# One core, one decoder block: the triangular inverse's upper two steps take two chunks in one product, and the decay masks come from GpSimd selections

## The chip, the cores and the metric

The kernel runs on one core of a Trainium2 chip. The metric is the device time of the whole program in microseconds (us). The time before is the median of three runs, 2971.11 us (2970.61 to 2977.27).

Engines: PE is TensorE (matrix products; PEld is its weight load), DVE is VectorE, ACT is ScalarE, POOL is GpSimd, SP issues the DMAs. Each runs its own instructions in order and waits on semaphores of the others.

## What is computed

A decoder trunk of one layer on 2048 tokens of width 1024: gated DeltaNet attention (8 heads of 128) and a 4-head attention over 256 memory tokens, side by side, then a squared-ReLU MLP, each with a residual and a layer norm. The change touches DeltaNet only. Cut to what matters:

```
gc = cumsum(g)                                     # within a chunk
decay = exp(where(causal, gc[:, None] - gc[None, :], -inf))
lower = where(strict, (beta * k) @ k.T * decay, 0)
a_mat = eye + lower
u = solve(a_mat, beta * v);  w = solve(a_mat, beta * k * exp(gc))
attn_qk = (q @ k.T) * decay
# then the scan over chunks with state S:
v_new = u - w @ S;  o = q_decay @ S + attn_qk @ v_new
S = S * exp(gc_last) + k_decay.T @ v_new
```

The reference uses chunks of 64 tokens. The kernel uses chunks of 128, which gives the same result, and needs the inverse of a unit lower triangular 128x128 matrix for every chunk and head.

## The kernel before

Tokens come in NB = 4 blocks of TB = 512, each of NC = 4 chunks of P = 128. For a block the kernel runs DeltaNet and memory attention, the output projection, norm 1, the MLP (its second product as a seven-product scheme on 2x2 blocks) and norm 2. Big products are in fp32r with each operand split into a high and a low part, three passes for one product (`mm3`). Weights are split by ACT (`CAST whl`) and DVE (`TENSOR_TENSOR whl`). Block 0 splits the input weights and stores them, the later blocks load them split.

DeltaNet is a pipeline over heads: at step t the kernel records `gdn_b(t-2)` (the scan with the state), `gdn_a(t-1)` (decay, k·k, q·k, the inverse) and `dense(t)` (the projections q, k, v, z, named aq, ak, av, az in the trace). In `gdn_a`, `gb` is a DMA that lays the row of cumulated gates over all partitions; DVE adds a mask (`m_l`, `m_at`: 0 or ±1e30) and ACT takes the exponential. This gives `dl` and `at`, which DVE multiplies with the products `pkq`.

`invert` gets `L` = `dl`, four chunks side by side. First DVE inverts the 16-row diagonal blocks by columns (`Xc`, `Bc`, `Lc`). Then three steps double the block: 16 to 32, 32 to 64 and 64 to 128 rows. Each step has two products with a copy between them, -X2 · L21 · X1:

- the first product goes into bank `pq`, ACT copies it to `Q`;
- the second, with the other inverse as stationary operand, goes into bank `pp`, and DVE (by scaling with -1) writes the result to its place.

Buffers: `XB`, `LB` (16 to 32), `L32`, `X32` (32 to 64), `L` itself and `X64` (64 to 128); `ZT` and `Z` hold the 32-row inverses, transposed and not; `Y` is the result, whose first reader is `pc<-R,Y` in `gdn_b`. In the two upper steps each of the four chunks is a product of its own with a stationary operand of 64 columns. The trace names a buffer without its number: L32 is `L`, X32 and X64 are both `X`.

All of this is only recorded. `Recorder.issue` then sets the order on all engines: it is a list scheduler that gives each operation a duration (`cost`) and picks, on the engine that is free first, the ready operation recorded first. So a change of costs or dependences moves instructions everywhere. All recorded instructions are issued from one line, L320. `rec.buf(..., bufs, ...)` limits how many tiles of a tag live at once; `.part(key)` says that parts of a tile are independent of each other.

Of the kernel before, what the change touches and what calls it, by code (L numbers as in the profile page):

```python
# [134 lines left out]
class Recorder:  # L135
# [47 lines left out]
    @staticmethod  # L183
    def cost(o, name, wr, rd, args, kw):
        e = o.eng
        shapes = [r.shape for r in wr] + [r.shape for r in rd]
        n = max([_prod(s[1:]) for s in shapes] or [1])
        if e == "PE":
            rhs = kw.get("rhs", args[2])
            mo, n = _prod(args[1].shape[1:]), _prod(rhs.shape[1:])  # L190
            f32 = name == "transpose" or isinstance(rhs, Ref) and rhs.buf.dtype == F32
            o.load = 4 + 0.84 * mo
            o.last = 2.4 + 0.8334 * n if f32 else 13.4 + 0.4167 * n
            if name == "transpose":
                return o.last
            if f32:
                return o.last + max(o.last, o.load)
            return o.last
        psum = any(r.buf.psum for r in rd + wr)
        if e == "SP":  # L200
            o.extra = 1700 + _prod(wr[0].shape if wr else rd[0].shape) * 4 / 300.0
            return 450
        scal = [v for v in args[2:] if isinstance(v, Ref)] if name.startswith("tensor_scalar") else []
        scal += [v for k, v in kw.items() if k in ("scalar", "scalar1", "scale", "bias") and not isinstance(v, (int, float))]
        if e == "ACT":
            n = _prod((wr[0]).shape[1:])
# [12 lines left out]

    def issue(self):  # L220
# [116 lines left out]
def hybrid_layer(  # L337
# [24 lines left out]
    nc = tc.nc  # L362
# [6 lines left out]
    cst = ctx.enter_context(tc.tile_pool(name="cst", bufs=1))  # L369
# [31 lines left out]
    m_at = cst.tile([P, P], F32, name="m_at")  # L401
    nc.gpsimd.memset(m_at, 0.0)
    m_l = cst.tile([P, P], F32, name="m_l")
    nc.gpsimd.memset(m_l, 0.0)
    nc.gpsimd.affine_select(out=m_at, in_=m_at, compare_op=ALU.is_ge, fill=-1e30,
                            base=0, pattern=[[1, P]], channel_multiplier=-1)
    nc.gpsimd.affine_select(out=m_l, in_=m_l, compare_op=ALU.is_gt, fill=1e30,
                            base=0, pattern=[[-1, P]], channel_multiplier=1)
# [19 lines left out]
    rec = Recorder(nc, tc)  # L428
    BN_DIM = nc.vector.BN_STATS_DIM
    nc = rec  # L430
# [154 lines left out]
    def gates(b, T):  # L585
# [26 lines left out]
        t = small("gt", sh, 1)  # L612
# [3 lines left out]
        d = small("gd", sh, 1)  # L616
# [6 lines left out]
        p = small("gp", sh, 1)  # L623
# [36 lines left out]
        gct = small("gct", [32, P], 2)  # L660
# [69 lines left out]
    def invert(L, par):  # L730

        Lq = small("Lq", [P, 32, NC], 2)
        for q in range(4):
            r = slice(32 * q, 32 * q + 32)
            nc.vector.tensor_copy(Lq[r].rearrange("p f c -> p c f"), L[r, :, 32 * q:32 * q + 32])
            nc.gpsimd.tensor_copy(inv[par % NI]["LB"][r, :, 32 * q:32 * q + 16], L[r, :, 32 * q:32 * q + 16])
        for p in range(2):
# [9 lines left out]
        for j in range(15):  # L747
# [3 lines left out]
                                    in1=Lc[:, j:j + 1].to_broadcast([P, w, NC]), op=ALU.mult)  # L751
# [7 lines left out]
        XB, LB, L32, X32, X64, Q = (inv[par % NI][n] for n in ("XB", "LB", "L32", "X32", "X64", "Q"))  # L759
        Y = slot("Y", "s%d" % par)  # L760
        Y3 = v4(Y)
        nc.gpsimd.memset(Y, 0.0)
# [2 lines left out]
            nc.scalar.copy(out=XB[r, :, r], in_=Z[r])  # L765

        W = P - 16
        pq = bank("pq", "ga%d" % par)[:W, :64].rearrange("p (c f) -> p c f", c=NC)
        for c in range(NC):
            nc.tensor.matmul(pq[:, c], LB[:, c, :W], ZT[:, c, 16:32], start=True, stop=True)  # L770
        nc.scalar.copy(out=Q[:W, :, :16], in_=pq)
        pp = bank("pp", "ga%d" % par)[:W, :64].rearrange("p (c f) -> p c f", c=NC)
        for c in range(NC):
            nc.tensor.matmul(pp[:, c], XB[:, c, :W], Q[:, c, :16], start=True, stop=True)
        nc.vector.tensor_tensor(out=ZT[:W, :, 16:32], in0=ZT[:W, :, 16:32], in1=pp, op=ALU.subtract)

        Z = small("Z32", [P, NC, 32], 2)
# [6 lines left out]
        pq = bank("pq", "ga%d" % par)[:64, :P].rearrange("p (c f) -> p c f", c=NC)  # L784
        for c in range(NC):
            nc.tensor.matmul(pq[:, c], L32[:, c], ZT[:, c], start=True, stop=True)
        nc.scalar.copy(out=Q[:64, :, :32], in_=pq)
        p32 = bank("pp", "ga%d" % par)
        pp = p32[:64, :P].rearrange("p (c f) -> p c f", c=NC)
        for c in range(NC):  # L790
            nc.tensor.matmul(pp[:, c], X32[:, c], Q[:, c, :32], start=True, stop=True)
        t32 = Lq[:32].rearrange("p f c -> p (f c)")
        nc.vector.transpose(t32, p32[:32, :P])
        for p in range(2):
            nc.vector.tensor_scalar_mul(Y3[64 * p:64 * p + 32, :, 64 * p + 32:64 * p + 64],
                                        pp[32 * p:32 * p + 32], -1.0)
        nc.vector.tensor_scalar_mul(X64[32:64, :, :32], t32.rearrange("p (c f) -> p c f", c=NC), -1.0)

        pq = bank("pq", "ga%d" % par)[:64, :2 * P].rearrange("p (c f) -> p c f", c=NC)
        for c in range(NC):  # L800
            nc.tensor.matmul(pq[:, c], L[:, c, :64], Y3[:, c, 64:], start=True, stop=True)
        nc.scalar.copy(out=Q[:64], in_=pq)
        pp = bank("pp", "ga%d" % par)[:64, :2 * P].rearrange("p (c f) -> p c f", c=NC)
        for c in range(NC):
            nc.tensor.matmul(pp[:, c], X64[:, c], Q[:, c], start=True, stop=True)
        nc.vector.tensor_scalar_mul(Y3[:64, :, 64:], pp, -1.0)
        return Y3

    def sumsq(p3, nm):
# [7 lines left out]
    def gdn_a(h, r, G):  # L817
# [23 lines left out]
        nc.vector.tensor_tensor(out=at3, in0=gb3, in1=m_at.unsqueeze(1).to_broadcast([P, NC, P]), op=ALU.add)  # L841
# [427 lines left out]
```

## Time and profile before

| | |
|---|---|
| median of the runs | 2971.11 us |
| profiled execution | 2967.86 us, its span 2966.1 us |
| granted TensorE clock | 0.998 |
| PE MATMUL pq<-ZT,L and pq<-Y,dl (first products of the two steps) | 256 passes each |
| PE MATMUL pp<-Q,X (their second products) | 512 passes |
| chain that ended last, by line | PE af 40%, PE ao 6%, PE pp 2%, PE pq 2% |

The span is the time from the first to the last instruction. A row of the timeline gives start, duration, engine, line, operation, output<-inputs and the shape; x8 merges eight instructions, and a bracket holds the idle time ahead of it and who ended it. A row of the groups gives count, busy us, mean ns, and the idle time ahead. An fp32 matmul shows as two passes per product. Matmuls are pipelined, so their durations overlap.

### The profile page before, as it was taken

How to read it: one execution, taken by the hardware profiler on the slowest of the kernel's cores; microseconds unless marked ns; L12 is line 12 of the kernel's file. 1: busy time of each engine (PE TensorE's matmuls, PEld its weight loads, DVE VectorE, ACT ScalarE, POOL GpSimd, SP SyncE). 2: the span in 40 equal slices, each digit the busy share in tenths (PEclk: the TensorE clock that was granted, in tenths of full speed). 3: DMA queues.
4: the chain of work that ended last, by engine and by line, in shares of the span. 5: the costliest groups of instructions: out<-in, count | busy, mean ns of one | idle time of the engine just before them, and what ended most of it. 6: DMA issues, size and time to landing. Idle time of an engine off the chain costs nothing.

```text
span 2966.1 us, 43768 instructions
## 1 busy us (share of the span) xinstructions
PE 2922.6 (99%) x15172; PEld 2410.1 (81%) x15172; DVE 2178.7 (73%) x5568; ACT 1518.2 (51%) x3582; POOL 342.1 (12%) x872
## 2 busy tenths in 40 slices
PE   8999999999999999999999999999999999999998
PEld 6888778888788878888888878888878887888886
DVE  7899887666888876665588777755668877675667
ACT  6666535444456652554545555344454556444443
POOL 2222100000122201000022220000001221000000
PEclk9999999999999999999999999999999999999999
DMA  8655577555733322544473333244456333324444
GB/s 283 238 192 178 192 237 234 194 190 181 278 136 121 121 100 79 158 146 137 154 258 135 122 111 100 89 144 148 149 168 244 125 122 111 100 86 149 145 146 135
DMA packets 127709, 469.84 MB, mean 158 GB/s; under 512 B 14464, under 2 KB 16896, under 8 KB 109056
## 3 DMA queue, kind: packets, MB, share of 16 engines
q1 hardware_dynamic: 126912, 467.00, 47.1%
q8 instruction: 119, 1.95, 0.3%
q14 instruction: 102, 0.84, 0.1%
q10 hardware_dynamic: 576, 0.06, 0.0%
HBM read 402.97 MB, written 64.03 MB: 157 GB/s over the span
## 4 chain that ended last, share of the span: by engine, by line
PE 81%; DVE 8%; ACT 7%; DMA 2%; issue 2%; POOL 1%; ACTq 0%; POOLq 0%; DVEq 0%
PE af L320 40%; PE ao L320 6%; PE az L320 5%; PE av L320 5%; PE ak L320 4%; PE aq L320 4%; PE amq L320 3%; PE pc L320 3%; DVE y L320 2%; PE pp L320 2%; PE pq L320 2%; PE po L320 2%; PE pkq L320 1%; DVE whl L320 1%; PE sps L320 1%
## 5 line engine op out<-in xcount | busy, mean ns | idle before, releaser
L320 DVE TENSOR_TENSOR whl<-wraw,whl 128x1024 fp32r<-128x1024 f32 (+1 forms) x446 | 541.4, 1216 | 462.6 <-ACT whl L320 460.9
L320 ACT CAST whl<-wraw 128x1024 fp32r<-128x1024 f32 (+1 forms) x446 | 466.6, 1046 | 371.7 <-PE af L320 202.6
L320 PE MATMUL af<-Thi,whl 128*128 128x512 f32 (+1 forms) x2304 | 649.8, 366 | 4.6 <-DVE whl L320 2.7
L320 PEld LDWEIGHTS af<-Thi,whl 128*128 128x128 f32 x2304 | 416.8, 189 | 76.0 <-DVE whl L320 3.7
L320 PE MATMUL af<-whl,xh 128*128 128x512 f32 x1536 | 474.8, 390 | 1.3 <-DVE whl L320 0.7
L320 PE MATMUL af<-Tlo,whl 128*128 128x512 f32 (+1 forms) x1152 | 421.1, 366 | 0.0
L320 PE MATMUL af<-whl,xl 128*128 128x512 f32 x896 | 346.0, 389 | 0.0
L320 PEld LDWEIGHTS af<-whl,xh 128*128 128x128 f32 x1536 | 287.8, 188 | 67.4 <-ACT whl L320 3.7
L320 PEld LDWEIGHTS af<-Tlo,whl 128*128 128x128 f32 x1152 | 217.3, 189 | 35.1
L320 PE MATMUL ao<-whl,ch 128*128 128x512 f32 x768 | 245.2, 397 | 0.3 <-DVE y L320 0.3
L320 ACT ACTIVATE rl<-af 128x512 f32<-128x512 f32 x128 | 76.5, 598 | 277.1 <-PE af L320 275.2
L320 PEld LDWEIGHTS af<-whl,xl 128*128 128x128 f32 x896 | 168.2, 188 | 34.4
L320 PE MATMUL aq<-Thi,whl 128*128 128x512 f32 x512 | 181.7, 412 | 7.2 <-ACT Thi L320 7.2
L320 PE MATMUL az<-Thi,whl 128*128 128x512 f32 x512 | 177.3, 406 | 1.1 <-DVE whl L320 1.1
L320 PE MATMUL av<-Thi,whl 128*128 128x512 f32 x512 | 176.6, 406 | 0.0
L320 PE MATMUL ak<-Thi,whl 128*128 128x512 f32 x512 | 173.5, 403 | 0.0
L320 PEld LDWEIGHTS ao<-whl,ch 128*128 128x128 f32 x768 | 143.1, 188 | 27.9 <-issue 1.4
L320 PE MATMUL ao<-whl,cl 128*128 128x512 f32 x384 | 156.2, 407 | 0.0
L320 DVE SCALAR_TENSOR_TENSOR y<-y,af 128x512 f32<-128x512 f32 x224 | 146.2, 677 | 8.7 <-PE af L320 8.7
L320 POOL MEMSET Y<- 128x512 f32 x32 | 16.8, 525 | 1037.9 <-PE af L320 921.0
L320 PEld LDWEIGHTS aq<-Thi,whl 128*128 128x128 f32 x512 | 94.7, 190 | 22.3 <-ACT Thi L320 7.2
L320 PEld LDWEIGHTS az<-Thi,whl 128*128 128x128 f32 x512 | 93.9, 189 | 17.3 <-DVE whl L320 1.5
(251 smaller groups left out, 5747.2 us busy)
## 6 DMA issues: line engine op xcount, KB each, us to landing
wraw<-in_w_ff_dram SPq DMA_DIRECT2D x224, 512.0 KB, 4.0
whl<-wsc SPq DMA_DIRECT2D x108, 1024.0 KB, 4.8
wraw<-tsc SPq DMA_DIRECT2D x128, 512.0 KB, 3.4
wsc<-whl SPq DMA_DIRECT2D x36, 1024.0 KB, 4.8
wraw<-in_w_out_dram SPq DMA_DIRECT2D x48, 512.0 KB, 4.2
wraw<-in_w_in_dram SPq DMA_DIRECT2D x35, 512.0 KB, 5.8
wq<-in_w_ff_dram SPq DMA_DIRECT2D x64, 256.0 KB, 4.4
tsc<-wq SPq DMA_DIRECT2D x64, 256.0 KB, 3.8
```

What stands on the lines that cost most here:

```text
L320: o.fn(*[res(a) for a in o.args], **{k: res(v) for k, v in o.kw.items()})
```

## The change

The two upper steps hold two chunks in one stationary operand of 128 columns with two diagonal blocks: chunk c in one block and chunk c + 2 in the other. So `L32`, `X32`, `X64` and the new `LP` (the lower left 64x64 blocks of L) are 128 columns wide and two deep. The moving operand has the two chunks on different partitions: `ZP` (in the space of `Lq`) for the first step, `YP` for the second. There are two products where there were four. Copies that filled one operand are split in halves between POOL and DVE, and results of `pp` between DVE and ACT. The masks `m_l` and `m_at` go; two POOL selections write `dl` and `at` from `gb`. Two POOL costs in the scheduler change, and `gct` has one buffer in place of two.

```
         if name == "tensor_copy":
-            return 119 + 3.34 * n
+            return 120 + 1.3 * n
+        if name == "affine_select":
+            return 180 + 0.9 * n
...
-        for n, f in (("XB", P), ("LB", P), ("L32", 64), ("X32", 64), ("X64", 64), ("Q", 64)):
-            d[n] = rec.buf(cst, (P, NC, f), F32, n + str(i), 1, n)
+        for n, shape in (("XB", (NC, P)), ("LB", (NC, P)), ("L32", (2, P)), ("X32", (2, P)), ("X64", (2, P)),
+                         ("LP", (2, P)), ("Q", (2 * P,))):
+            d[n] = rec.buf(cst, (P,) + shape, F32, n + str(i), 1, n)
...
         for p in range(2):
-            nc.gpsimd.tensor_copy(inv[par % NI]["L32"][64 * p + 32:64 * p + 64, :, 32 * p:32 * p + 32],
-                                  L[64 * p + 32:64 * p + 64, :, 64 * p:64 * p + 32])
+            rows = slice(64 * p + 32, 64 * p + 64)
+            nc.gpsimd.tensor_copy(L32[rows, :, 64 * p:64 * p + 32].part((0, p)), L[rows, 0:2, 64 * p:64 * p + 32])
+            nc.vector.tensor_copy(L32[64 * p:64 * p + 32, :, 64 * p + 32:64 * p + 64].part((1, p)),
+                                  L[rows, 2:4, 64 * p:64 * p + 32])
+        nc.gpsimd.tensor_copy(LP[64:, :, :64].part(0), L[64:, 0:2, :64])
+        nc.vector.tensor_copy(LP[:64, :, 64:].part(1), L[64:, 2:4, :64])
...
+        for p in range(2):
+            odd = slice(64 * p + 32, 64 * p + 64)
+            nc.vector.tensor_copy(ZP[64 * p:64 * p + 32].part(2 * p + 1), ZT[odd, 2:4])
+            nc.scalar.copy(out=ZP[odd].part(2 * p), in_=ZT[odd, 0:2])
         nc.vector.transpose(Z.rearrange("p c f -> p (c f)"), ZT.rearrange("p c f -> p (c f)"))
         for p in range(2):
-            nc.vector.tensor_copy(X32[32 * p:32 * p + 32, :, 32 * p:32 * p + 32], Z[64 * p:64 * p + 32])
-            nc.gpsimd.tensor_copy(X64[32 * p:32 * p + 32, :, 32 * p:32 * p + 32], Z[32 * p:32 * p + 32])
+            for u, eng in ((0, nc.gpsimd), (1, nc.vector)):
+                q = quads[2 * p + u]
+                eng.tensor_copy(X32[q, :, q].part((u, p)), Z[64 * p:64 * p + 32, 2 * u:2 * u + 2])
...
-        for c in range(NC):
-            nc.tensor.matmul(pq[:, c], L32[:, c], ZT[:, c], start=True, stop=True)
+        for c in range(2):
+            nc.tensor.matmul(pq[:, c], L32[:, c], ZP[:, c].part(0, 1, 2, 3), start=True, stop=True)
...
-        for c in range(NC):
-            nc.tensor.matmul(pq[:, c], L[:, c, :64], Y3[:, c, 64:], start=True, stop=True)
-        nc.scalar.copy(out=Q[:64], in_=pq)
+        YP = small("YP", [P, 2, 64], 1)
+        nc.vector.tensor_copy(YP[:64].part(1), Y3[64:, 2:4, 64:])
+        nc.scalar.copy(out=YP[64:].part(0), in_=Y3[64:, 0:2, 64:])
+        for c in range(2):
+            nc.tensor.matmul(pq[:, c], LP[:, c], YP[:, c], start=True, stop=True)
+        nc.scalar.copy(out=Q[:, P:].rearrange("p (c f) -> p c f", c=2).part(2), in_=pq)
...
-        nc.vector.tensor_scalar_mul(Y3[:64, :, 64:], pp, -1.0)
+        nc.vector.tensor_scalar_mul(Y3[:64, 2:4, 64:], pp[64:], -1.0)
+        nc.scalar.activation(Y3[:64, 0:2, 64:], pp[:64], AF.Copy, scale=-1.0)
...
-        nc.vector.tensor_tensor(out=dl3, in0=gb3, in1=m_l.unsqueeze(1).to_broadcast([P, NC, P]), op=ALU.add)
+        nc.gpsimd.affine_select(out=dl3, in_=gb3, compare_op=ALU.is_gt, fill=1e30,
+                                base=0, pattern=[[0, NC], [-1, P]], channel_multiplier=1)
```

Two places show how the change moves instructions. The first is PE in block 1, head 2: the end of its 32-to-64 step and its 64-to-128 step, before:

```order
L320 MATMUL pp<-Q,X_157 64x32 x4
L320 MATMUL av<-Thi,whl 128x512
L320 MATMUL av<-Tlo,whl 128x512
L320 MATMUL av<-Thi,whl 128x512 x2
L320 MATMUL av<-Tlo,whl 128x512
L320 MATMUL av<-Thi,whl 128x512
L320 MATMUL pq<-Y,dl 64x64 x4
L320 MATMUL av<-Thi,whl 128x512
L320 MATMUL av<-Tlo,whl 128x512
L320 MATMUL av<-Thi,whl 128x512
L320 MATMUL pp<-Q,X_162 64x64 x4
```

And PE now, at the 64-to-128 step of the same head:

```order
L322 MATMUL ak<-Tlo,whl 128x512
L322 MATMUL ak<-Thi,whl 128x512
L322 MATMUL av<-Thi,whl 128x512
L322 MATMUL av<-Tlo,whl 128x512
L322 MATMUL av<-Thi,whl 128x512
L322 MATMUL pq<-YP,LP 128x64 x2
L322 MATMUL av<-Thi,whl 128x512
L322 MATMUL av<-Tlo,whl 128x512
L322 MATMUL av<-Thi,whl 128x512
L322 MATMUL pp<-Q,X_152 128x64 x2
```

Four products of 64 columns are two of 128; between the two steps stand eleven rows of projection where five stood, and from the last product to the first reader of Y (pc<-R,Y) it is 18 rows where it was 14.

The second place is POOL, where the selections for a head stand ahead of the copies of the head before it, again in block 1; before:

```order
L320 TENSOR_TENSOR vbs<-betah,rk 128x4
L320 TENSOR_TENSOR bh<-beta,rk 128x4
L320 MEMSET Y 128x512
L320 TENSOR_TENSOR bh<-bh,rk 128x4
L320 TENSOR_TENSOR nbe<-bh,neg 128x4
L320 COPY X_162<-Z_9944 32x4x32 x2
```

And POOL now:

```order
L322 AFFINE_SELECT dl<-gb 128x512
L322 AFFINE_SELECT at<-gb 128x512
L322 MEMSET Y 128x512
L322 TENSOR_SCALAR ss<-ss 128x8
L322 TENSOR_SCALAR m_10098<-oss 128x4
L322 TENSOR_TENSOR rk<-ss,mhalf 128x4
L322 TENSOR_TENSOR m_10098<-m_10098,e_9226 128x4
L322 COPY X_147<-Z_10114 32x2x32
L322 TENSOR_TENSOR ro<-m_10098,mhalf 128x4
L322 COPY X_147<-Z_10114 32x2x32
L322 COPY X_152<-Z_10114 32x2x32 x2
```

The two selections have come in ahead of Y's memset, and the copies of X now hold X32's first half (X_147), which stood on DVE, besides X64's (X_152).

More of the change, by code (lines that the diff above doesn't have):

```diff
@@ L400, in hybrid_layer @@
                             base=0, pattern=[[1, P]], channel_multiplier=-1)
[L401 to L408, printed above, removed]
     half = cst.tile([P, 2], F32, name="half")
@@ L659, in gates @@
         nc.tensor.transpose(pt[:32, :P], gcf, ident)
[L660 removed]
+        gct = small("gct", [32, P], 1)
         nc.vector.tensor_copy(gct, pt[:32, :P])
@@ L758, in invert @@
         nc.vector.transpose(ZT.rearrange("p c f -> p (c f)"), Z.rearrange("p c f -> p (c f)"))
-        XB, LB, L32, X32, X64, Q = (inv[par % NI][n] for n in ("XB", "LB", "L32", "X32", "X64", "Q"))
+        XB, LB, X32, X64, Q = (inv[par % NI][n] for n in ("XB", "LB", "X32", "X64", "Q"))
         Y = slot("Y", "s%d" % par)
@@ L767, in invert @@
         W = P - 16
+        Q16 = Q[:W, :64].rearrange("p (c f) -> p c f", c=NC).part(0)
         pq = bank("pq", "ga%d" % par)[:W, :64].rearrange("p (c f) -> p c f", c=NC)
@@ L770, in invert @@
             nc.tensor.matmul(pq[:, c], LB[:, c, :W], ZT[:, c, 16:32], start=True, stop=True)
-        nc.scalar.copy(out=Q[:W, :, :16], in_=pq)
+        nc.scalar.copy(out=Q16, in_=pq)
         pp = bank("pp", "ga%d" % par)[:W, :64].rearrange("p (c f) -> p c f", c=NC)
         for c in range(NC):
-            nc.tensor.matmul(pp[:, c], XB[:, c, :W], Q[:, c, :16], start=True, stop=True)
+            nc.tensor.matmul(pp[:, c], XB[:, c, :W], Q[:, c * 16:(c + 1) * 16].part(0), start=True, stop=True)
@@ L779, in invert @@
         for p in range(2):
-            nc.vector.tensor_copy(X32[32 * p:32 * p + 32, :, 32 * p:32 * p + 32], Z[64 * p:64 * p + 32])
-            nc.gpsimd.tensor_copy(X64[32 * p:32 * p + 32, :, 32 * p:32 * p + 32], Z[32 * p:32 * p + 32])
+            for u, eng in ((0, nc.gpsimd), (1, nc.vector)):
+                q = quads[2 * p + u]
+                eng.tensor_copy(X32[q, :, q].part((u, p)), Z[64 * p:64 * p + 32, 2 * u:2 * u + 2])
+        for p in range(2):
+            for u, eng in ((0, nc.gpsimd), (1, nc.vector)):
+                q = quads[2 * u + p]
+                eng.tensor_copy(X64[q, :, q].part((u, p)), Z[quads[p], 2 * u:2 * u + 2])
@@ L792, in invert @@
[L792 to L800, printed above, removed]
-            nc.tensor.matmul(pq[:, c], L[:, c, :64], Y3[:, c, 64:], start=True, stop=True)
@@ L802, in invert @@
-        nc.scalar.copy(out=Q[:64], in_=pq)
-        pp = bank("pp", "ga%d" % par)[:64, :2 * P].rearrange("p (c f) -> p c f", c=NC)
-        for c in range(NC):
-            nc.tensor.matmul(pp[:, c], X64[:, c], Q[:, c], start=True, stop=True)
-        nc.vector.tensor_scalar_mul(Y3[:64, :, 64:], pp, -1.0)
+        pq = bank("pq", "ga%d" % par)[:, :64].rearrange("p (c f) -> p c f", c=2)
+        for c in range(2):
+            nc.tensor.matmul(pq[:, c], L32[:, c], ZP[:, c].part(0, 1, 2, 3), start=True, stop=True)
@@ new lines, in invert @@
+        nc.scalar.copy(out=Q[:, 64:P].rearrange("p (c f) -> p c f", c=2).part(1), in_=pq)
+        pb = bank("pp", "ga%d" % par)[:, :64]
+        pp = pb.rearrange("p (c f) -> p c f", c=2)
+        for c in range(2):
+            nc.tensor.matmul(pp[:, c], X32[:, c], Q[:, 64 + c * 32:64 + (c + 1) * 32].part(1), start=True, stop=True)
+        tr = Lq.rearrange("p f c -> p (f c)")[:64, 64:].part("t")
+        nc.vector.transpose(tr, pb[:64])
+        for p in (1, 0):
+            o = Y3[64 * p:64 * p + 32, :, 64 * p + 32:64 * p + 64]
+            nc.vector.tensor_scalar_mul(o[:, 2:4], pp[quads[2 * p + 1]], -1.0)
+            nc.scalar.activation(o[:, 0:2], pp[quads[2 * p]], AF.Copy, scale=-1.0)
@@ new lines, in invert @@
+        tr = tr.rearrange("p (c f) -> p c f", c=2)
+        for u in range(2):
+            nc.vector.tensor_scalar_mul(X64[quads[2 * u + 1], :, quads[2 * u]].part((u, 2)), tr[quads[u]].part("t"), -1.0)
+        YP = small("YP", [P, 2, 64], 1)
+        nc.vector.tensor_copy(YP[:64].part(1), Y3[64:, 2:4, 64:])
+        nc.scalar.copy(out=YP[64:].part(0), in_=Y3[64:, 0:2, 64:])
+        pq = bank("pq", "ga%d" % par)[:, :P].rearrange("p (c f) -> p c f", c=2)
+        for c in range(2):
+            nc.tensor.matmul(pq[:, c], LP[:, c], YP[:, c], start=True, stop=True)
@@ L807, in invert @@
+        nc.scalar.copy(out=Q[:, P:].rearrange("p (c f) -> p c f", c=2).part(2), in_=pq)
+        pp = bank("pp", "ga%d" % par)[:, :P].rearrange("p (c f) -> p c f", c=2)
+        for c in range(2):
+            nc.tensor.matmul(pp[:, c], X64[:, c], Q[:, P + c * 64:P + (c + 1) * 64].part(2), start=True, stop=True)
+        nc.vector.tensor_scalar_mul(Y3[:64, 2:4, 64:], pp[64:], -1.0)
+        nc.scalar.activation(Y3[:64, 0:2, 64:], pp[:64], AF.Copy, scale=-1.0)
         return Y3
@@ L840, in gdn_a @@
         at3 = v4(at)
-        nc.vector.tensor_tensor(out=at3, in0=gb3, in1=m_at.unsqueeze(1).to_broadcast([P, NC, P]), op=ALU.add)
+        nc.gpsimd.affine_select(out=at3, in_=gb3, compare_op=ALU.is_ge, fill=-1e30,
+                                base=0, pattern=[[0, NC], [1, P]], channel_multiplier=-1)
         for c in range(NC):
```

7 lines of the change are left out of this document (2 added, 5 removed).

## The prediction

> **What bounds the kernel now.** I read the page first, then stretches of time, then the timeline of single products.
>
> ```profile
> span 2966.1 us, 43768 instructions
> PE 2922.6 (99%) x15172; PEld 2410.1 (81%) x15172; DVE 2178.7 (73%) x5568; ACT 1518.2 (51%) x3582; POOL 342.1 (12%) x872
> PE 81%; DVE 8%; ACT 7%; DMA 2%; issue 2%; POOL 1%; ACTq 0%; POOLq 0%; DVEq 0%
> ```
>
> TensorE is busy for 2922.6 of 2966.1 us and holds 81% of the chain that ended last. So time that leaves TensorE leaves the kernel, as long as another engine doesn't hold the stage. The stage that is changed is DeltaNet, at four places, one for each block of 512 tokens:
>
> ```profile
> 130.00:300.00 170.00, 167.99 (x1018) 137.61 (x1017) 153.79 (x555) 115.25 (x365) 44.89 (x121) 1.00 0.52 179
> 800.00:1080.00 280.00, 278.50 (x1643) 229.77 (x1643) 225.39 (x881) 166.51 (x564) 64.26 (x187) 1.00 0.35 124
> 1560.00:1800.00 240.00, 236.97 (x1427) 193.93 (x1426) 190.24 (x752) 138.71 (x477) 56.14 (x155) 0.99 0.32 115
> 2290.00:2540.00 250.00, 246.92 (x1486) 202.22 (x1484) 200.66 (x799) 146.32 (x503) 54.15 (x141) 1.00 0.32 113
> ```
>
> The columns after the stretch are PE, weight loads, DVE, ACT, POOL, granted clock, DMA share and GB/s. PE is full in all four (277 of 280 us and alike). But DVE is busy for 153.79 of 170 us (90%) in block 0, which still splits its weights into high and low parts, and for 79 to 80% in the other three. ACT is at 58 to 68%, POOL at 22 to 26%.
>
> "Busy" on PE hides something, since durations of matmuls overlap. What a product really takes is read from the starts around it. Here are PE's rows of one head in block 1, around a 32-to-64 product and a 64-to-128 product of before:
>
> ```profile
> 911.81 0.40 PE L320 MATMUL av<-Thi,whl 128*128 128x512 f32 x1
> 912.14 0.65 PE L320 MATMUL pq<-ZT,L 128*64 128x32 f32 x8
> 912.72 0.50 PE L320 MATMUL av<-Thi,whl 128*128 128x512 f32 x1
> 913.06 0.40 PE L320 MATMUL av<-Tlo,whl 128*128 128x512 f32 x1
> 913.29 0.40 PE L320 MATMUL av<-Thi,whl 128*128 128x512 f32 x1
> ...
> 916.17 0.40 PE L320 MATMUL av<-Thi,whl 128*128 128x512 f32 x1
> 916.49 0.68 PE L320 MATMUL pq<-Y,dl 128*64 128x64 f32 x8
> 917.10 0.50 PE L320 MATMUL av<-Thi,whl 128*128 128x512 f32 x1
> 917.44 0.40 PE L320 MATMUL av<-Tlo,whl 128*128 128x512 f32 x1
> ```
>
> A projection's pass takes 0.23 us (913.06 to 913.29). From the pass ahead of a group to the second one behind it lie 1.25 us (911.81 to 913.06) and 1.27 us (916.17 to 917.44); less two passes of 0.23, the groups take **0.79 and 0.81 us**. x8 is four chunks in two fp32 passes each. The loads show how little of that is work:
>
> ```profile
> 912.14 0.54 PEld L320 LDWEIGHTS pq<-ZT,L 128*64 128x64 f32 x8 [0.36 <-DVE Bc L320]
> 919.18 0.59 PEld L320 LDWEIGHTS ptv<-ident,cv 128*128 128x128 f32 x4
> 919.18 0.39 PE L320 MATMUL az<-Thi,whl 128*128 128x512 f32 x1
> 919.41 0.60 PE L320 MATMUL ptv<-ident,cv 128*128 128x128 f32 x4
> 919.77 0.47 PE L320 MATMUL az<-Thi,whl 128*128 128x512 f32 x1
> 920.08 0.39 PE L320 MATMUL az<-Tlo,whl 128*128 128x512 f32 x1
> ```
>
> The eight 64-column loads start with their group (912.14), though the pass ahead started at 911.81; the four 128-column loads of ptv start at 919.18, together with the pass ahead, and are hidden under it. One 64-column load lasts 0.138 us in the groups below, so the eight start 0.057 us apart ((0.54-0.138)/7), 0.46 us in all. The other 0.33 us are edges: the array is run dry on entry and on the way back. The 128-wide group of four passes takes 919.18 to 920.08 = 0.90 us, less 0.46: **0.44 us**, without edges. A product of 128 columns with two passes says the same:
>
> ```profile
> 947.43 0.39 PE L320 MATMUL ak<-Thi,whl 128*128 128x512 f32 x1
> 947.66 0.38 PE L320 MATMUL pc<-R,Y 128*128 128x128 f32 x2
> 947.80 0.48 PE L320 MATMUL ak<-Thi,whl 128*128 128x512 f32 x1
> 948.11 0.39 PE L320 MATMUL ak<-Tlo,whl 128*128 128x512 f32 x1
> ```
>
> 0.68 us less 0.46 is 0.22 for two passes, 0.44 for four.
>
> **The change part by part: PE.** Each head loses four 64-column groups of eight passes (two at 0.79, two at 0.81 us) and gets four 128-column groups of four passes. Their moving operand is 32 or 64 wide, so the loads set the pass: twice 0.057, four times, is 0.46; the rows above give 0.44. I take 0.45. Gain: 2 x 0.34 + 2 x 0.36 = **1.40 us a head**, 44.8 us for 32 heads (4 blocks of 8):
>
> ```profile
> L320 PEld LDWEIGHTS pq<-ZT,L x256: 132/138/232, 102.0 to 2548.7; 128*64 128x64 f32 x128
> L320 PE MATMUL pp<-Q,X x512: 213/222/271, 104.3 to 2554.5; 128*64 128x64 f32 x86, 128*64 128x32 f32 x85
> ```
>
> 256 passes are 32 heads of eight. The 112-column groups of the 16-to-32 step stay as they are.
>
> A rule speaks against this: the Trainium skill, "TensorE: Matmul & The Clock Gate", section "LDWEIGHTS (loading the stationary operand)", has the load as columns / 1.2 ns, so by its figures, as an estimate, eight 64-column loads and four 128-column ones are both 0.43 us and nothing is won. The 0.057 us above agrees with it per load. The skill's "TensorEngine Tiling (Array Packing)", "Key Properties", says that going from one tiling mode to another drains TensorE, and counts 128x64 as a mode of its own; the late loads at 912.14 agree. By the first rule alone the sum would be 0, by both 44.8 us.
>
> **DVE.** These rows go or shrink:
>
> ```profile
> L320 DVE TENSOR_TENSOR dl<-gb,m_l 128x512 f32<-128x512 f32 x32 | 21.8, 682 | 0.1
> L320 DVE TENSOR_TENSOR at<-gb,m_at 128x512 f32<-128x512 f32 x32 | 21.8, 683 | 0.2 <-PE pc L320 0.2
> L320 DVE COPY X<-Z 32x128 f32<-32x128 f32 x64 | 15.5, 242 | 1.1
> L320 DVE STREAM_TRANSPOSE Lq<-pp 32x128 f32<-32x128 f32 x32 | 9.7, 302 | 18.2 <-PE pp L320 18.1
> L320 DVE TENSOR_SCALAR Y<-pp 32x128 f32<-32x128 f32 x64 | 16.9, 263 | 0.7
> L320 DVE TENSOR_SCALAR X<-Lq 32x128 f32<-32x128 f32 x32 | 7.3, 229 | 0.6
> L320 DVE TENSOR_SCALAR Y<-pp 64x256 f32<-64x256 f32 x32 | 13.3, 415 | 12.4 <-PE pp L320 11.9
> ```
>
> Out go 2 x 0.68 for the masks and, in the steps, 2 x 0.242 + 0.302 + 2 x 0.263 + 0.229 + 0.415 = 1.96: 3.32 us. In come ten SBUF copies (two L32, one LP, two ZP, two X32, two X64, one YP). Most move half of the 0.242 us row's elements; between a mere fixed part and the whole row I take 0.22, so 2.2. With the narrower transpose (0.27), two Y at 0.22, two X64 scalings at 0.20 and the last Y at 0.29 that is 3.6. DVE **gains 0.3 us a head** (bounds -0.2 to +0.6). In blocks 1 to 3 a fifth of DVE is free, which hides it. In block 0, 16.2 of 170 us are free: a head takes some 35 us (eight in the second stretch's 280), so 3.3 us are free per head, and 1.40 + 0.3 eat half of them. There I count on half the gain.
>
> **ACT and POOL.**
>
> ```profile
> L320 ACT COPY Y<-ZT 32x128 f32<-32x128 f32 x128 | 37.7, 295 | 19.4 <-DVE ZT L320 17.8
> L320 ACT COPY vt<-pc 128x128 f32<-128x128 f32 x128 | 34.2, 267 | 126.2 <-PE pc L320 125.7
> L320 POOL COPY X<-Z x64: 279/285/1318, 102.1 to 2549.4; 32x128 f32<-32x128 f32 x64
> L320 POOL MEMSET Y<- 128x512 f32 x32 | 16.8, 525 | 1037.9 <-PE af L320 921.0
> L407 POOL TENSOR_SCALAR_AFFINE_SELECT m_l<-m_l 128x128 f32<-128x128 f32 x1 | 0.3, 292 | 0.0
> ```
>
> ACT gets two ZP, one YP and three Y pieces, 0.25 to 0.27 us each by the first two rows, less narrower Q copies: about 1.4 us on some 24 busy of 35 in block 0 (115.25 of 170). Free time hides that. POOL gets two selections per head. A 128x128 one took 0.292 us; four times the elements is 0.29 (all fixed) to 1.17 us (all per element). The 128x512 memset took 0.525 us, so I take 0.6, 1.2 for both. POOL is three quarters free, and in the order shown the selections stand well ahead of the products they feed. The masks' wait for gb moves from DVE's queue to POOL's. Behind it stand Y's memset and the ss/rk scaling of the next head; these had the slack of POOL's free time so far.
>
> What is late next is the inversion's own chain. Two copy stages are new in it (ZP ahead of the first product, YP ahead of the third), 0.25 us each, and X32's first half now comes from POOL. The order has the last product 18 rows ahead of its first reader pc<-R,Y (14 before), so most is covered by projection passes. I charge 0.15 us of new PE wait per head; bounds 0 (all hidden) and 0.6 (both stages and their hand-overs exposed).
>
> **Sum**, against the profiled execution's 2967.86 us: blocks 1 to 3, 24 x 1.40 = 33.6, less 24 x 0.15 = 3.6; block 0, half of 8 x 1.40 = 5.6. Gain 35.6, so 2932.3. The runs' median is 2971.11, 3.3 above; on it I forecast **2936 us**, 1.2% less.
>
> **Rivals.** (1) *Loads only*: the edges come from the semaphore wait ahead of each group, not from its width, and stay. Against it: pc<-R,Y waits for DVE's R as well and has no edge. PE then gains nothing: 2971. (2) *The other engines hold the stage*: block 0 gives nothing since DVE is full, and in blocks 1 to 3 the whole 0.6 us of the new stages shows: 24 x 0.80 = 19.2, less DVE's 0.3 x 8 = 2.4 in block 0. That gives 2954. For it: 7% of the chain on ACT, 8% on DVE. (3) *Slower, by X32 on POOL*: the second product of the 32-to-64 step now waits for two POOL copies of Z. They took 0.285 us in the median but 1.318 at most. If they ran at 1.3 each, 2.6 us would stand against the 1.1 us that the first product (0.45), Q's copy and their hand-overs cover; with 0.24 for the transpose that is 1.75 us of wait a head. It decides from 1.40 on: 32 x 0.35 = 11, so 2982. Against it: a median near the minimum. The skill's "GPSIMD Engine Reference", section "Specifications", names VectorE's two-port modes and its two-input instructions as sharing the SBUF interface; the 1.318 us agree, though nothing in this trace shows the cause.
>
> **How the numbers follow.** Forecast 0.68, (1) 0.07, (2) 0.20, (3) 0.05. The forecast's own range runs from everything gained (2971 - 45 = 2926, and up to 6 us of the 43.5 us that PE idles now, since another order may lose fewer) to half its waits more. I put 2920 to 2957, which takes in (2) and leaves out (1) and (3). About 0.3%, 9 us, is what a measurement of this kernel tells from no change. Faster 0.88, same 0.07, slower 0.05.
>
> **What would show it.** Right: groups "128*128 128x32 x4" and "128x64 x4" whose neighbours stand 0.45 + 0.46 us apart, loads hidden under the pass ahead, PE's passes down by 512, DVE over 93% busy in block 0. Wrong: edges that stay, PE waits on POOL X or ACT YP of over 0.3 us a head, or a DeltaNet stage as long as before.

## The result, and the profile after

| | before | after |
|---|---|---|
| median of the runs | 2970.86 us (2968.97 to 2977.27, 4 runs) | 3010.55 us (3007.82 to 3013.75, 4 runs) |
| profiled execution | 2967.86 us | 3008.75 us |

The ratio is 1.013, with an interval of 1.0111 to 1.0149. The change makes the kernel 40 us slower where 35 us less had been forecast.

The page of the kernel after, engine totals and the chain that ended last by engine:

```profile
span 3007.0 us, 43426 instructions
PE 2907.9 (97%) x14660; PEld 2401.7 (80%) x14660; DVE 2220.4 (74%) x5792; ACT 1562.0 (52%) x3774; POOL 380.9 (13%) x1029
PE 68%; DVE 18%; ACT 7%; issue 3%; POOL 2%; DMA 2%; DVEq 0%; POOLq 0%; ACTq 0%; SPq 0%
```

PE has its 512 passes less and is busy for 15 us less, but the span is 41 us longer. PE's share of the chain fell from 81 to 68%, and DVE's rose from 8 to 18%. The same four stretches of DeltaNet show where (columns after the stretch: PE, weight loads, DVE, ACT, POOL, granted clock, DMA share, GB/s):

```profile
130.00:300.00 170.00, 160.46 (x905) 132.86 (x903) 152.58 (x564) 119.64 (x394) 50.48 (x144) 0.99 0.50 175
800.00:1080.00 280.00, 266.98 (x1472) 220.27 (x1472) 226.14 (x869) 170.07 (x589) 73.72 (x216) 0.99 0.38 136
1560.00:1800.00 240.00, 226.62 (x1264) 187.91 (x1264) 201.41 (x810) 144.91 (x504) 62.62 (x193) 0.99 0.35 125
2290.00:2540.00 250.00, 235.37 (x1307) 195.25 (x1306) 205.24 (x815) 149.55 (x520) 63.12 (x183) 0.99 0.35 127
```

PE, which was full (278.50 of 280), now idles 13 of 280 us in block 1. DVE is hardly fuller than before there (226.14 against 225.39), so the stage isn't short of DVE's time.

Below, *length* is DeltaNet's time in a block on PE, from the last pass of one MLP to the first pass of the next, and *stall* is length less PE's work. The work counts each pass at what it takes between undisturbed neighbours (0.227 us for 512 columns in fp32r, an fp32 pass the longer of its load and its stream), plus 0.32 us for the edges of a 64-column group. It is a model and holds to a few us; the lengths are measured.

| block | 0 | 1 | 2 | 3 |
|---|---|---|---|---|
| length before, us | 430.8 | 386.5 | 390.5 | 389.1 |
| length after | 445.7 | 396.7 | 396.8 | 397.9 |
| PE's work before / after | 408.9 / 398.1 | 378.3 / 367.2 | 378.3 / 367.2 | 378.3 / 367.2 |
| stall before / after | 21.9 / 47.6 | 8.2 / 29.4 | 12.2 / 29.6 | 10.8 / 30.7 |

By this model the work falls by 44 us over the four blocks, as forecast, and the stall rises by 84. Now PE in block 1, head 2 of the kernel after, with DVE and ACT beside it, in the timeline:

```profile
925.39 0.63 PE L322 MATMUL ak<-Thi,whl 128*128 128x512 f32 x2
...
925.86 0.53 PE L322 MATMUL pp<-Q,X 128*128 128x32 f32 x4
...
926.22 0.48 PE L322 MATMUL ak<-Tlo,whl 128*128 128x512 f32 x1
...
926.54 0.63 PE L322 MATMUL ak<-Thi,whl 128*128 128x512 f32 x2
...
927.63 0.69 DVE L322 SCALAR_TENSOR_TENSOR cq<-th,cq 128x512 f32<-128x512 f32 x1
...
928.24 0.23 DVE L322 STREAM_TRANSPOSE Lq<-pp 64x64 f32<-64x64 f32 x1
...
928.51 0.23 DVE L322 TENSOR_SCALAR Y<-pp 32x64 f32<-32x64 f32 x1
...
929.00 0.22 ACT L322 ACTIVATE Y<-pp 32x64 f32<-32x64 f32 x1
...
929.30 0.39 PE L322 MATMUL av<-Thi,whl 128*128 128x512 f32 x1
...
929.84 0.68 DVE L322 TENSOR_TENSOR kq<-cq,kq 128x512 fp32r<-128x512 f32 x1
930.55 0.22 DVE L322 TENSOR_SCALAR Y<-pp 32x64 f32<-32x64 f32 x1
...
930.80 0.21 ACT L322 ACTIVATE Y<-pp 32x64 f32<-32x64 f32 x1 [1.58 <-DVE Y L322]
...
931.04 0.29 ACT L322 COPY YP<-Y 64x128 f32<-64x128 f32 x1
931.28 0.22 DVE L322 COPY YP<-Y 64x128 f32<-64x128 f32 x1
...
931.62 0.52 PEld L322 LDWEIGHTS pq<-YP,LP 128*128 128x128 f32 x4 [2.36 <-ACT YP L322]
```

The group itself is as forecast: from 925.39 to 926.54 lie 1.15 us with three projection passes of 0.23, which leaves **0.46 us** for pp, without edges. But its result is ready at about 926.4 and DVE takes it at 928.24, since it is behind with other work. Then four pieces of Y run in turns, DVE, ACT, DVE, ACT, and two copies to YP follow. PE starts its last projection pass at 929.30 and has nothing until 931.62. From pp to pq it is 5.8 us; before it was 2.18 for the same head, from this row to pq at 916.49:

```profile
914.31 0.65 PE L320 MATMUL pp<-Q,X 128*64 128x32 f32 x8
```

The waits of PE's weight loads over the whole kernel after (us in total, times, longest):

```profile
PEld pq L322 <- ACT YP L322: 26.1, 20, 2.4
PEld pc L322 <- DVE R L322: 15.9, 21, 1.9
PEld ptv L322 <- ACT Y L322: 12.6, 20, 1.7
PEld ptq L322 <- ACT kd L322: 11.5, 14, 2.4
PEld pp L322 <- ACT Q L322: 10.7, 18, 1.4
PEld pc L322 <- DVE state L322: 9.1, 17, 1.4
```

And the same waits before:

```profile
PEld pp L320 <- ACT Q L320: 9.5, 15, 1.0
PEld ptq L320 <- ACT kd L320: 5.3, 14, 1.7
PEld pc L320 <- DVE state L320: 3.2, 6, 0.8
PEld pc L320 <- DVE R L320: 2.3, 8, 0.4
PEld ptv L320 <- DVE Y L320: 1.0, 2, 0.6
```

The largest is the new copy stage, but over half of the rise in these rows stands at products that the change doesn't touch (pc, ptv, ptq). PE is ahead of the others at many places, not only at YP.

### The profile page after: what moved, and what is told of

The parts are those of the page before. It is cut to its first block, busy times and chain, and to the rows that moved or that the text cites. A ratio compares the mean times of both kernels' runs of the same rounds, so it can differ in the third digit from the quotient of the medians.

```text
span 3007.0 us, 43426 instructions
## 1 busy us (share of the span) xinstructions
PE 2907.9 (97%) x14660; PEld 2401.7 (80%) x14660; DVE 2220.4 (74%) x5792; ACT 1562.0 (52%) x3774; POOL 380.9 (13%) x1029
## 4 chain that ended last, share of the span: by engine, by line
PE 68%; DVE 18%; ACT 7%; issue 3%; POOL 2%; DMA 2%; DVEq 0%; POOLq 0%; ACTq 0%; SPq 0%
PE af L322 40%; PE ao L322 6%; PE az L322 4%; PE av L322 3%; PE aq L322 2%; DVE y L322 2%; PE pc L322 2%; DVE cq L322 2%; PE ak L322 2%; PE amq L322 2%; DVE whl L322 1%; DVE Lq L322 1%; PE po L322 1%; ACT jq L322 1%; DVE dl L322 1%
## 5 line engine op out<-in xcount | busy, mean ns | idle before, releaser
L322 DVE SCALAR_TENSOR_TENSOR y<-y,af 128x512 f32<-128x512 f32 x224 | 146.5, 678 | 10.1 <-PE af L322 10.1
L322 PEld LDWEIGHTS av<-Thi,whl 128*128 128x128 f32 x512 | 96.4, 191 | 17.3
```

The source lines that it names most:

```text
L322: o.fn(*[res(a) for a in o.args], **{k: res(v) for k, v in o.kw.items()})
```

## The experiments

**1 and 2: masks or steps.** One kernel puts only the masks of the change into the kernel before, the other takes only the masks out of the kernel after (two mask additions on DVE again; scratch tiles of the squares are in bf16 to make room).

```
+        if name == "affine_select":
+            return 180 + 0.9 * n
...
-        nc.vector.tensor_tensor(out=at3, in0=gb3, in1=m_at.unsqueeze(1).to_broadcast([P, NC, P]), op=ALU.add)
+        nc.gpsimd.affine_select(out=at3, in_=gb3, compare_op=ALU.is_ge, fill=-1e30,
+                                base=0, pattern=[[0, NC], [1, P]], channel_multiplier=-1)
```

Masks alone:

> The kernel before, with the masks put in by the two POOL selections (and their cost in the scheduler), the inverse's steps as before. Theory A (the longer chain of the two steps makes TensorE wait) expects no loss here: DVE is freed of 1.36 us a head, so 2960 to 2973 us. Theory B (the selections on POOL hold up the copies and the beta factors behind them, or share DVE's port) expects most of the loss here: over 2990 us, with waits for POOL on the chain.

Measured: 2973.27 us (2970.90 to 2976.66, 10 runs) against 2970.75, ratio 1.0007 (0.9998 to 1.0017). That is the upper end of theory A's range, and no loss shows from the masks.

Steps alone:

> The changed kernel with the masks back on DVE (one as a product of the triangle with 1e30 plus gb, one as before; the squares' scratch tiles are bf16 to make room). Theory A expects the loss to stay or grow: 3005 to 3035 us, with pq<-YP, pc<-R,Y and ptv waiting as in the changed kernel. Theory B expects 2925 to 2950 us.

Measured: 3003.02 us (3001.46 to 3004.47), ratio 1.011 (1.0093 to 1.0127), 2 us under theory A's range. The wait of pq's loads at YP is still there (32.1 us, 26.1 in the kernel after). The loss lies in the steps, with what goes with them: this kernel keeps the new costs of POOL's copies and the single `gct`, and neither was tried alone.

**3 and 4: the scheduler's durations.** The order is a plan made from `cost`. The groups of DVE and ACT in the kernel after show what the small operations really take (count, busy us, mean ns, idle before):

```profile
L322 DVE COPY Lq<-dl 32x128 f32<-32x128 f32 x128 | 40.1, 313 | 2.2
L322 DVE COPY X<-Z 32x64 f32<-32x64 f32 x128 | 27.4, 214 | 2.7
L322 DVE TENSOR_SCALAR Y<-pp 32x64 f32<-32x64 f32 x64 | 14.2, 222 | 2.0
L322 DVE COPY L<-dl 32x64 f32<-32x64 f32 x64 | 12.6, 197 | 0.9
L322 ACT ACTIVATE Y<-pp 32x64 f32<-32x64 f32 x64 | 13.7, 213 | 42.2 <-DVE Y L322 41.1 <-PE sps L322 0.6
L322 ACT COPY YP<-Y 64x128 f32<-64x128 f32 x32 | 9.4, 295 | 0.7
```

By `cost` these are 135, 101, 135 (68 + 1.042 x 64), 101, 105 (52 + 0.833 x 64) and 201 ns: about 0.1 us too short each. Over all operations of the inversion on 64 partitions or fewer, DVE is planned 2.3 us a head too short in the kernel after and 1.2 in the one before (counts times the difference of mean and plan), ACT 1.4 and 0.95. POOL's copies go the same way, since the change lowers their cost: planned 0.45 us a head too long before, 0.85 too short after. No run put that cost back alone; PE's loads wait for POOL only 6.2 us in the whole kernel after, so its direct share is small. On PE it is the other way round: `cost` knows no edges, so by this reading PE ran 4 x 0.33 us a head behind its own plan before, together with the others; now it keeps its plan and they don't. Both kernels get one line:

```
+        part = 110 if e in ("ACT", "DVE") and wr[0].shape[0] <= 64 else 0
...
-            return 68 + (0.52 if fast else 1.042) * n + 62 * len(scal) + (7 * n if name == "reciprocal" else 0)
+            return part + 68 + (0.52 if fast else 1.042) * n + 62 * len(scal) + (7 * n if name == "reciprocal" else 0)
```

(and the same for ACT). Nothing that is computed changes, only the order. After:

> The changed kernel with one edit to the scheduler's costs: DVE and ACT operations whose output starts on at most 64 partitions cost 110 ns more (in the trace of the kernel before the next operation started 230 to 310 ns after such a one, where the scheduler counts 101 to 201). Theory A1 (the order calls the products of the two steps too early, because it counts the small copies too short) expects PE's waits ahead of pq<-YP, ptv and pc<-R to fall by half or more, and 2935 to 2975 us. Theory A2 (the chain and its hand-overs are too long whatever the order) expects the waits to stay within a fifth: over 2995 us.

Measured: 2949.76 us (2947.22 to 2951.65), ratio to the kernel before 0.9932 (0.9917 to 0.9947): **61 us less** than the kernel after. The loads' wait at ptv falls from 12.6 to 2.9 us, that at pc for R only from 15.9 to 10.1. PE's share of the chain and its wait for YP in this kernel:

```profile
PE 73%; DVE 15%; ACT 5%; POOL 2%; issue 2%; DMA 2%; POOLq 0%; DVEq 0%; ACTq 0%; SPq 0%
...
PEld pq L323 <- ACT YP L323: 5.9, 12, 0.7
```

The same line in the kernel before:

> The kernel before with the same edit to the costs, as the control of that edit. A1 expects little, since its TensorE waited for only some 40 us in all: 2955 to 2975 us. If it gains as much as the changed kernel does, the edit says nothing on the change.

Measured: 2956.11 us (2955.87 to 2957.63), ratio 0.9955 (0.994 to 0.997), 15 us less. So the old plan called PE too early in both, and mending it is worth four times as much in the kernel after. At equal costs the change is worth -6 us, not +40; DeltaNet of blocks 1 to 3 is 381.5 us with it and 385.7 without, block 0 is 435.7 and 429.6.

**5 to 7: the chain of copies.** YP is written straight from pp (its diagonal blocks by POOL, early), so that the copies out of Y go.

```
+        nc.vector.tensor_scalar_mul(YP[0:32, :, 32:64].part((1, 2)), pp[quads[3]], -1.0)
+        nc.scalar.activation(YP[64:96, :, 32:64].part((0, 2)), pp[quads[2]], AF.Copy, scale=-1.0)
...
-        YP = small("YP", [P, 2, 64], 1)
-        nc.vector.tensor_copy(YP[:64].part(1), Y3[64:, 2:4, 64:])
-        nc.scalar.copy(out=YP[64:].part(0), in_=Y3[64:, 0:2, 64:])
```

At the scheduler's own costs:

> The changed kernel at its own costs, with YP written straight from the products instead of by copies out of Y: POOL copies YP's diagonal blocks early from ZT, DVE and ACT write its two other blocks from pp ahead of the pieces of Y. Between the 32-to-64 product and the 64-to-128 one there is then one copy stage where four pieces of Y, in turns on DVE and ACT, and two copies of them stood. The waits of pq for YP were 14.8 us (DVE) and 26.1 us (ACT). Theory H (the hand-over chain from pp by Y to YP is what PE waits for): most of these 41 us go and the time is 2965 to 2990. Theory O (only the scheduler's order matters: durations in its plan too short, so it calls PE too early however long the chain is): the scheduler moves pq up by what the chain became shorter, PE waits at pq or a little later (ptv, pc<-R) as before, and the time is 2995 to 3012.

Measured: 3014.89 us (3012.81 to 3016.28), ratio 1.0144 (1.0129 to 1.0159), a little above the ranges of both theories. The timeline of PE for the same head, in this kernel:

```profile
922.30 0.40 PE L322 MATMUL ak<-Thi,whl 128*128 128x512 f32 x1
924.92 0.66 PE L322 MATMUL pq<-YP,LP 128*128 128x64 f32 x4 [2.22 <-ACT Y L322]
```

YP was written by 922.87, yet pq waits until the last piece of Y at 924.65: there is one bank for pp and pq of a head parity, and the pieces of Y still read pp. So this edit shortened the chain less than meant: from pp to pq it is 3.9 us in the mean of the 32 heads, where it was 4.4. The order took at least as much out of PE: it puts 2.3 us of other products between the two, where it put 3.0 (starts in the traces, 0.23 us for a pass of 512 columns and 0.11 for a narrower one). So PE waits as long as before.

With the 110 ns of experiment 3:

> The kernel of e5 with the longer durations of e3 in the scheduler (110 ns more for DVE and ACT operations on 64 partitions or fewer). e3 took 2949.8. Theory H (the chain still costs PE in e3's order): 2932 to 2944, DeltaNet of blocks 1 to 3 at about 375 to 378 us (381.5 in e3). Theory O (with fitting durations the order hides the chain whatever its length, and what is left in e3 is something else): 2946 to 2952. Theory D (DVE full in block 0 is what is left): block 0 stays at 433 to 436 us (435.7 in e3) even if the others become shorter.

Measured: 2945.05 us (2943.83 to 2946.97), ratio 0.9908 (0.9892 to 0.9925), between the two theories. Blocks 1 to 3 are no shorter than in experiment 3 (383.0 against 381.5); block 0 is 10 us shorter (426.0), against theory D.

With DVE's three copies out of L on POOL as well:

> The kernel of e6 with DVE's three copies out of L (two halves of L32 and one of LP, 2 x 0.197 and 0.289 us = 0.68 us a head) on POOL. Theory D (DVE holds block 0): 8 x 0.68 = 5.5 us less DVE work there, so block 0 is 4 to 6 us shorter than in e6, the others 0 to 1 us, and the time 4 to 8 us below e6. Rival (PE waits for the chain, not for DVE's sum of work): within 2 us of e6, or longer by 3 to 10 us if the copies now stand late in POOL's queue behind the selections.

Measured: 2953.97 us (2953.15 to 2956.89), ratio 0.9941 (0.9927 to 0.9956), 9 us more. Block 0 stays at 426.5, so freeing DVE gains nothing there; that the copies came late in POOL's queue and ate the gain is not excluded.

**8 to 10: a plan that is later still.** 220 ns in place of 110, in three kernels. After:

> The changed kernel with 220 ns in place of e3's 110 ns on the planned duration of DVE and ACT operations on 64 partitions or fewer. e3 took 2949.8 and left 14 us of stall in DeltaNet of blocks 1 to 3 each and 38 us in block 0, against 7 and 21 in the kernel before with the same costs (e4). Theory O (PE is still called too early; the starts of such operations lie 60 to 145 ns further apart than even 110 ns more than the first plan gives at some, and hand-overs between engines are planned at nothing): the stalls fall towards those of e4 and the time to 2925 to 2942. Rival C (plan fits by now; the stalls left are work that really doesn't fit, DVE's sum in block 0 and the inversion's chain): 2946 to 2956, or longer, since a plan that is too slow puts the chain's steps too far back.

Before:

> Control: the kernel before with the same 220 ns. With 110 it took 2956.1, and 43 us of stall are left in it. Theory O: little is to be had, since its products' edges of 0.33 us already make PE late: 2950 to 2958. Rival C: the same or up to 6 us longer. The difference to e8 says what the change of the steps is worth when the plan is late enough for both.

YP straight from pp:

> The kernel of e6 (YP straight from the products) with 220 ns in place of 110. e6 took 2945.1. Theory O: 2922 to 2938. Rival C: 2943 to 2952. If e8 and this one agree within 4 us, the length of the chain from pp to YP is of no account with either plan.

(A remark in the first of these was wrong: the scheduler does plan hand-overs, 160 ns from DVE and 165 from ACT.) Measured: 2958.37 us (ratio 0.9956, 0.9942 to 0.997), 2954.90 (0.9949, 0.9934 to 0.9964) and **2934.95** (2933.82 to 2935.46; 0.9881, 0.9866 to 0.9895). The two theories each got one of the two changed kernels: 8.6 us longer where the copies are in the chain, 10.1 shorter where they are not. The first loses its time in block 0 (440.1 us against 435.7 in experiment 3; the granted clock was 0.88 between 300 and 400 us) and in the MLP behind it; its blocks 1 to 3 stay at 381.1. Without the copies they fall to 376.5. So the length of the chain counts after all, once the plan is late enough. In the last kernel the head looks as it was meant to, in PE's timeline:

```profile
925.67 0.39 PE L323 MATMUL ak<-Tlo,whl 128*128 128x512 f32 x1
925.90 0.55 PE L323 MATMUL pq<-YP,LP 128*128 128x64 f32 x4
926.26 0.70 PE L323 MATMUL ak<-Thi,whl 128*128 128x512 f32 x2
926.80 0.40 PE L323 MATMUL ak<-Tlo,whl 128*128 128x512 f32 x1
927.04 0.55 PE L323 MATMUL pp<-Q,X 128*128 128x64 f32 x4
```

From pp of the first step (922.01) to pq are 3.9 us, with projections to the last of them. DeltaNet of blocks 1 to 3 is 376.5 us against 384.7 in experiment 9: 8.2 of the 11.1 us of work that the change removes from PE arrive. Block 0 is 434.2 against 430.9, and the loss is in one place of it, the end of the stage, here in 20 us stretches:

```profile
300.00:320.00 20.00, 20.00 (x107) 16.98 (x106) 18.39 (x71) 13.26 (x44) 3.17 (x11) 1.00 0.52 179
320.00:340.00 20.00, 17.16 (x104) 14.67 (x103) 14.47 (x63) 14.78 (x52) 8.18 (x21) 0.92 0.15 47
340.00:360.00 20.00, 15.93 (x74) 12.89 (x73) 16.64 (x77) 7.35 (x22) 1.84 (x7) 0.74 0.42 144
360.00:380.00 20.00, 17.84 (x96) 13.78 (x94) 18.20 (x64) 11.82 (x38) 4.34 (x9) 1.00 0.70 243
```

Up to 320 us PE is full, with DVE at 18.39 of 20. In the 60 us behind it PE idles 9 us and the granted clock falls to 0.74; experiment 9 is busy for 59.1 of these 60 us, and experiment 6, the same kernel with 110 ns, for 58.5. So the later plan loses this, not the kernel's work: it leaves 3 passes of the memory attention's projection (amq) between 320 and 360 us, where experiment 6 has 41. That these would have filled the gaps is not shown.

**11 and 12: the pieces of Y side by side.** The four pieces are marked as independent, so DVE's two and ACT's two no longer take turns.

```
-            nc.vector.tensor_scalar_mul(o[:, 2:4], pp[quads[2 * p + 1]], -1.0)
-            nc.scalar.activation(o[:, 0:2], pp[quads[2 * p]], AF.Copy, scale=-1.0)
+            nc.vector.tensor_scalar_mul(o[:, 2:4].part((1, p)), pp[quads[2 * p + 1]], -1.0)
+            nc.scalar.activation(o[:, 0:2].part((0, p)), pp[quads[2 * p]], AF.Copy, scale=-1.0)
```

On the kernel after, at its own costs:

> The changed kernel at its own costs; only the four pieces of Y that are written out of the 32-to-64 product are marked as parts independent of each other. In the changed kernel they ran in turns, DVE, ACT, DVE, ACT, each waiting for the one before (ACT sat idle 41.1 us ahead of its pieces until DVE's was done); now DVE writes its two and ACT its two side by side. This is the cleaner test of the chain, since in e5 the bank of pp, of which there is one, still kept pq behind all four pieces. Theory H (hand-overs between the pieces are what PE waits for): PE's waits at pq<-YP of about 45 us fall by half or more, 2975 to 2992. Theory O (PE is called too early whatever the length of the chain, as the scheduler takes out of the plan what is taken out of the chain): 2998 to 3012.

Measured: 2993.32 us (2992.24 to 2993.96), ratio 1.0077 (1.0062 to 1.0092): 17 us less, between the two theories. PE's waits at pq in it:

```profile
PE pq L322 <- DVE YP L322: 22.2, 20, 2.1
...
PEld pq L322 <- ACT YP L322: 24.8, 22, 2.6
```

They did not fall (14.8 and 26.1 in the kernel after). From pp to pq it is now 2.8 us in the mean, 1.6 less, but the order puts only 1.6 us of other products between them, 1.4 less. The gain comes at other products (the loads of pc wait 14.3 us for `state` and R, before 25.0), perhaps since their makers no longer stand behind a piece of Y that waits. On the kernel of experiment 10:

> The kernel of e10 (YP straight from the products, 220 ns) with the same independent pieces, which frees the bank of pp earlier. e10 took 2935.0, with 9 us of stall in DeltaNet of blocks 1 to 3 each, and 36 us in block 0, of which 16 lie between 320 and 360 us, at the end of DeltaNet, where PE's granted clock fell as well (0.93 between 300 and 400 us). Theory H: blocks 1 to 3 fall from 376.5 to 373 to 375 us, 2925 to 2932. Theory O: the same within 4 us, 2931 to 2939. If the end of block 0 runs as in e6 (426.0 us against 434.2) another 8 us go, under either.

Measured: 2940.20 us (2937.10 to 2942.14), ratio 0.9898 (0.9881 to 0.9915), 5 us more than experiment 10 and just above both ranges; blocks 1 to 3 are 378.6. Here the turns cost nothing.

## Why the prediction was wrong

- **PE's gain: right.** It counted 0.45 us for a group of four passes; 0.46 was measured, in the timeline above and in the median of 31 groups of pp between projections. The passes fall by 512. The work falls by 44 us, against 44.8; that figure is the model's, with the edges put in. Rival 1 (loads only) is refuted. The rule of the Trainium skill ("TensorEngine Tiling (Array Packing)", "Key Properties") that a change of tiling mode drains TensorE agrees with these runs, in which a group of 0.79 to 0.81 us became one of 0.46; the load rule of its "TensorE: Matmul & The Clock Gate", "LDWEIGHTS (loading the stationary operand)", doesn't when it is taken alone, since it gave no gain on PE.
- **The step that failed is the charge for new waits: 0.15 us a head, bounds 0 and 0.6.** Measured is a rise of the stall by 84 us, 2.6 a head; blocks 1 to 3 lost 25 us where 30 were to be gained. The wait for ACT's YP alone, 0.8 us a head, is over the 0.3 that the prediction named as a sign of being wrong. Both ends of the bounds came from the new chain alone (two copy stages with their hand-overs), and the cover from counting rows: "the last product 18 rows ahead of its first reader". But the rows are placed by a plan with durations, and rows of cover say nothing if the engine that should use the time runs behind its plan. The reading that was left out was to set `cost` against the measured mean of each added operation. Experiments 3 and 4 show this cause by its removal: one line of durations takes 61 us off the kernel after and 15 off the one before, so 46 us of the difference between the two go with it. The orders show it as well: between pp and pq the kernel after puts 3.0 us of other products, which with pp's own 0.45 leaves about 1 of the 4.4 us empty in the mean head; in experiment 3 it is 3.7 of 4.1, in experiment 10 3.4 of 3.9, and with the 0.45 nothing is left empty.
- The chain got longer than the two stages, too: Y's four pieces take turns on two engines. Taking the turns away alone gives less: 17 us in experiment 11.
- Why the old kernel bore the same durations better is an inference: its PE was held back 1.3 us a head by unplanned edges. Its DVE and ACT were also less far behind the plan (1.2 and 0.95 us a head against 2.3 and 1.4). Both fit experiment 4, but no run put the edges back alone.
- **DVE: +0.3 us a head forecast, +1.3 measured** (2178.7 to 2220.4 us). The listed operations come to 3.5 us in and 3.3 out, close to the 3.6 and 3.32 forecast. Some 20 us of the rest are operations that the change doesn't touch and that got longer (last section). That DVE's sum was not the limit shows in experiments 3 and 6: DVE is still busy for 2203 and 2207 us there, yet 61 and 66 us of the kernel after's time are gone.
- **Block 0 at half of the gain since DVE is 90% busy: wrong reason.** It lost 15 us, with DVE at 152.58 of 170 us, 90% and not over 93. In experiment 6 it is 10 us shorter than in experiment 3 with the same work on DVE, and experiment 7 freed DVE and gained nothing there; in experiment 10 the loss stands at the end of the stage.
- **Masks and ACT's load: right.** Experiment 1 has the masks at 2.5 us, within its interval of no change. ACT is busy for 1.37 us a head more, against 1.4. POOL's selections took 0.75 and 0.69 us in the mean, against 0.6.
- **Rival 2** had the right kind of mechanism (waits for the other engines) and the wrong price: 0.6 us a head at most. **Rival 3** (X32 on POOL) didn't show: loads of pp waited 3.4 us for POOL's X in the whole kernel.

The likeliest time of the prediction, 2936 us, comes out with later durations and YP straight from pp (2934.95 us), the version that beats both kernels by the most. That is luck: with the same durations the kernel before takes 2954.90, so the change is worth 20 us there and not 35.

## What to carry over

When the order comes from a scheduler's durations, set its planned time of each new operation against the profile's mean before counting what hides it; many small operations on few partitions, each 0.1 us too short, put an engine 2 us behind in every round. If a change makes the bounding engine faster, it may also take away an unplanned delay that kept the plan true for the others, so calibrate the plan and run the old kernel with it as a control. A scheduler can take a shorter chain out of the plan again, so that the wait stays, and a buffer that exists once (here a bank) can keep the old chain in place.

## What the hardware showed

POOL's selections slow down DVE. The operation `Xc<-Xc,Bc` (two inputs, same code in all kernels), min, median and max in ns, before:

```profile
L320 DVE TENSOR_TENSOR Xc<-Xc,Bc x480: 119/189/272, 74.7 to 2543.0; 128x16 f32<-128x16 f32 x32, 128x28 f32<-128x28 f32 x32, 128x40 f32<-128x40 f32 x32, 128x52 f32<-128x52 f32 x32
```

after:

```profile
L322 DVE TENSOR_TENSOR Xc<-Xc,Bc x480: 124/190/670, 77.0 to 2582.3; 128x4 f32<-128x4 f32 x32, 128x16 f32<-128x16 f32 x32, 128x28 f32<-128x28 f32 x32, 128x40 f32<-128x40 f32 x32
```

with the steps alone (no selections):

```profile
L322 DVE TENSOR_TENSOR Xc<-Xc,Bc x480: 119/188/245, 77.1 to 2578.7; 128x4 f32<-128x4 f32 x32, 128x16 f32<-128x16 f32 x32, 128x28 f32<-128x28 f32 x32, 128x40 f32<-128x40 f32 x32
```

The median stays, and the longest goes from 0.27 to 0.67 us only where the selections run (0.678 with the masks alone). All 17 that take over 0.3 us in the kernel after lie beside a selection for nearly their whole length; five others that overlap one take 0.17 to 0.22 us, so not every one is held up. The Trainium skill, "GPSIMD Engine Reference", "Specifications", has VectorE's two-input instructions share the SBUF interface with GpSimd, and these rows agree.

A second surprise is the granted clock in experiment 10: 0.92 between 320 and 340 us and 0.74 between 340 and 360, where PE idled 2.8 and 4.1 us with no wait over 2.4, and 1.00 before and behind. The passes beside the waits pay for it; the same four of sps, at full clock and then at the lower one:

```profile
311.92 1.02 PE L323 MATMUL sps<-mq 128*128 128x256 f32 x4
341.47 1.91 PE L323 MATMUL sps<-mq 128*128 128x256 f32 x4
```

So a stall can be paid for twice. How much of block 0's loss that is was not tried, and idle time alone doesn't tell when: in experiment 3 PE idles 4.7 us between 340 and 360 us at 1.00, and the clock is 0.83 in the 20 us behind.
